# A planner that orders a two-layer trunk: later readiness times for TensorE's operands and for buffers in layer 1, and later first GpSimd transfers

## The chip, the cores and the metric

The kernel runs on one core of a Trainium2 chip. The metric is device time in microseconds of one execution, as a median over runs. The engines are called as in the profile: PE (TensorE, matmuls), PEld (its weight loads), DVE (VectorE), ACT (ScalarE), POOL (GpSimd) and SP (SyncE, which issues most transfers).

## What is computed

Two layers over 512 rows of 1024 features. Each layer is an adaptively modulated norm, a mixer with one input projection, a SiLU gate, an output projection and a gated residual. Layer 0 mixes by retention (4 heads), layer 1 by forgetting attention (16 heads of 64). A last RMS norm closes the trunk. The reference, cut to this:

```
for i in range(DEPTH):                      # DEPTH = 2
    shift, scale, gate = split(silu(c) @ mod_w[i] + mod_b[i], 3)
    h = rms_norm(x, norm_g[i]) * (1 + scale) + shift
    y = retention(h, ...) if i % 3 == 0 else forgetting_attention(h, ...)
    x = x + gate * y
return rms_norm(x, final_g)

# forgetting_attention, for each block of 128 queries
q = rms_norm(q, q_gain) * HD**-0.5;  k = rms_norm(k, k_gain)
cum = cumsum(log_sigmoid(f + b_f))
logits = q @ k.T + cum[q] - cum[k]          # causal
o = softmax(logits) @ v
y = (o * silu(g)) @ w_out
```

## The kernel before

The work is written as a program of operations (`trunk`), but it isn't emitted in the order in which it is written. Every call on an engine goes through `Proxy` and `Sched.add`, which makes a `Task` with its engine, its dependences on earlier tasks (found from the parts of buffers that are read and written), an estimated `cost` and a priority. The priority is TensorE's summed cost so far plus an offset that the program sets with `at`. When all tasks exist, `Sched.order` plays them through an event model and records the order in which they start; `emit` then issues the instructions in this order, all from line 472. On the chip each engine works through its own queue in that order, and semaphores hold what isn't ready. So the model's times decide only the order on each engine and which buffer slot a tile gets; a wait on the chip lasts as long as it really lasts.

The model, in `order`:

- Each engine takes, of its ready tasks, the one of lowest priority number whose new buffers fit. A task becomes ready when its last dependence is done plus a latency: `LAT` = 0.2 us across engines, 0 on TensorE itself, 0.13 us on another engine itself.
- Buffers are slots of a few physical pools: 60 of 512 columns ("C"), 14 of 1024 ("B"), 4 of 2048 ("G"), 24 tiny ones ("T") and the 8 PSUM banks ("Z"). Each kind of buffer has its own limit, for instance 4 banks of kind `r` (transposes, scores, values of a head) and 6 of kind `p` (projections). A slot is free again at the moment in which the last user ends.
- Costs are formulas, such as 0.069 + n / 960 us for VectorE on two inputs, 0.052 + n / 1200 (and 0.042 for a source in SBUF) for ScalarE, and n / 2260 for a matmul of n columns. A matmul of over 192 columns costs double in the model if fewer than 3072 columns were streamed in the tick (3.41 us) before.
- A transfer issued by POOL begins 0.6 us after its issue has ended, and one after the other: it is done 1.4 us and its bytes at 360 GB/s later. Transfers by SP share one modelled stream.
- In the opening, TensorE gets filler matmuls of constant ones (`filler`, tile `s` from `ones_r`) whenever it has nothing ready, until the first real product needs that bank. The fillers are real instructions on the chip.

The program around it: POOL first loads `crow` (the vector c), `vrow` (norm gains and modulation biases, three transfers) and `inv`. TensorE transposes `crow` for `csilu` and `vrow` for `vecs`, then x, and the first modulation weights are multiplied as they land; the first q and k projections of layer 0 follow. Layer 0's heads and output projection take up to about 400 us. Then come layer 1's norm, its projections of v, q and k, and the heads.

A head of layer 1 goes from engine to engine: `stacks` transposes the normalised q and k (`qn`) into PSUM, ScalarE and VectorE make stacked operands `st` from it (POOL copies some of them across partitions), `scores` multiplies them, VectorE adds the mask and the forget term (`lg`, with `ck`), ScalarE takes the exponential, POOL scales, `turn` transposes the probabilities, ScalarE and VectorE split them in two parts (`ph`), and `values` multiplies them with v into `oT`. `merge` and `zip2` interleave these steps with the remaining projections (tile `p`), whose weights come as `raw` and are split into `wh` (ScalarE) and `wl` (VectorE); `h2`, the normalised input, has the name `big`. `merge` sets the priorities only; the planner decides. After the last head, 192 matmuls of the output projection follow (tile `a`), and the final norm.

Of the kernel before, what the change touches and what calls it, by code (L numbers as in the profile page):

```python
# [26 lines left out]
PE = mybir.EngineType.PE  # L27
# [34 lines left out]

GATE1 = "q k v g0"

LOOK = 30.0

LAST = (1, 2, 3)
# [1 line left out]
N_C, N_B = 60, 14  # L69

START, TICK, TICK_COLS = 0.65, 10.24 / 3, 3072
KINDS = {
# [124 lines left out]
class Sched:  # L197
# [117 lines left out]
    def order(self):  # L315

        import heapq
        tasks = self.tasks
        free = {k: list(range(n)) for k, (n, _) in self.phys.items()}
        used = {k: 0 for k in self.kinds}  # L320
        turn = {k: 0 for k in self.kinds}
        avail = {e: [] for e in self.ENG.values()}
        busy = {e: True for e in avail}
        ev, count, out, table = [(START, 0, -i, e, None) for i, e in enumerate(busy)], 0, [], None
        hw = dma = reach = 0.0
        soft, soft_wait, soon = [], [], []
        ticks = {-1: 0}
        left = sum(t.eng == "PE" for t in tasks)
        for t in tasks:
            t.wait, t.ready = len(t.deps), 0.0  # L330
            if not t.wait:
                heapq.heappush(avail[t.eng], (t.prio, t.seq, t))

        def fits(t):
            if t.eng == "SP" and t.prio > reach:
                return False
            need = {}
            t.new = [b for b in t.bufs if b.slot is None and b.kind is not None]
            for b in t.new:
                ph, cap = self.kinds[b.kind]  # L340
                need[ph] = need.get(ph, 0) + 1
                if turn[b.kind] != b.seq or used[b.kind] >= cap or len(free[ph]) < need[ph]:
                    return False
            return True

        now = 0.0
        while True:
            moved = True
            while moved:
                moved = False  # L350
                for e in avail:
                    if busy[e]:
                        continue
                    held, got = [], None
                    while avail[e]:
                        x = heapq.heappop(avail[e])
                        if fits(x[2]):
                            got = x[2]
                            break
                        held.append(x)  # L360
                    for x in held:
                        heapq.heappush(avail[e], x)
                    if got is not None and e == "DVE" and now < LOOK and any(
                            x.prio < got.prio - 1.0 and x.ready < now + 0.2 and fits(x) for x in soon):
                        heapq.heappush(avail[e], (got.prio, got.seq, got))
                        continue
                    if got is None and e == "PE" and now > 1.5 and self.idle is not None and self.idle.buf.slot is not None:

                        got = self.filler()
                    if got is None:  # L370
                        continue
                    moved = True
                    if self.idle is not None and e == "PE" and not got.filler and self.idle.buf in got.bufs:
                        self.idle = None
                    for b in got.new:
                        ph = self.kinds[b.kind][0]
                        b.slot = free[ph].pop(0)
                        used[b.kind] += 1
                        turn[b.kind] += 1
                    out.append(got)  # L380
                    got.start = now
                    if e == "PE":
                        tick = int(now / TICK)
                        if ticks.get(tick - 1, 0) < TICK_COLS and got.cols > 192:
                            got.cost *= 2.0
                        tick = int((now + got.cost) / TICK)
                        ticks[tick] = ticks.get(tick, 0) + got.cols
                    if e == "PE":
                        left -= not got.filler or got is self.first
                        reach = max(reach, got.prio) if left else now + 1e9  # L390
                    busy[e] = True
                    count += 1
                    end = now + got.cost
                    if got.table not in (None, table):
                        end += 1.3
                        table = got.table
                    heapq.heappush(ev, (end, 0, count, e, None))
                    if got.bytes:
                        if e == "POOL":
                            soft.append(got)  # L400
                            a = end + 0.6
                        else:
                            hw = max(hw, now + 0.05) + 0.45
                            a = hw + 0.6
                        heapq.heappush(ev, (a, 3, count, None, got))
                    else:
                        got.done = end
                        heapq.heappush(ev, (end, 1, count, None, got))
            if not ev:
                break  # L410
            now = ev[0][0]
            while ev and ev[0][0] <= now:
                _, what, _, e, t = heapq.heappop(ev)
                if what == 0:
                    busy[e] = False
                elif what == 3 and t.eng == "POOL" and t is not soft[0]:

                    soft_wait.append(t)
                elif what == 3:
                    dma = max(now, dma) + t.bytes / 360e3  # L420
                    t.done = dma + 0.5
                    if t.eng == "POOL":
                        t.done = now + t.bytes / 360e3 + 1.4
                    count += 1
                    heapq.heappush(ev, (t.done, 1, count, None, t))
                elif what == 1:
                    if t.bytes and t.eng == "POOL":
                        soft.pop(0)
                        if soft and soft[0] in soft_wait:
                            count += 1  # L430
                            soft_wait.remove(soft[0])
                            heapq.heappush(ev, (now, 3, count, None, soft[0]))
                    for b in t.bufs:
                        b.users -= 1
                        if b.users == 0 and b.kind is not None:
                            free[self.kinds[b.kind][0]].append(b.slot)
                            used[b.kind] -= 1
                    for s in t.next:
                        lat = self.LAT if t.eng != s.eng else 0.0 if t.eng == "PE" else 0.13
                        s.ready = max(s.ready, t.done + lat)  # L440
                        s.wait -= 1
                        if not s.wait:
                            count += 1
                            heapq.heappush(ev, (s.ready, 2, count, None, s))
                            if s.eng == "DVE":
                                soon.append(s)
                else:
                    if t in soon:
                        soon.remove(t)
                    heapq.heappush(avail[t.eng], (t.prio, t.seq, t))  # L450
        if ev or any(avail.values()):
            todo = {e: [(t.emit[1], [(b.kind, b.seq) for b in t.new]) for _, _, t in sorted(avail[e])[:4]]
                    for e in avail}
            raise RuntimeError(f"stuck at {now:.1f} of {len(tasks) - len(out)} tasks: {todo}, {used}, {turn}")
        self.end = now
        return out
# [98 lines left out]
def trunk(tc, x, c, positions, mod_w, mod_b, norm_g, ret_w_in, ret_w_out, fox_w_in, fox_b_f,  # L555
# [6 lines left out]
    with ExitStack() as es:  # L562
# [5 lines left out]
        psp = es.enter_context(tc.tile_pool(name="psp", bufs=1, space=PSUM))  # L568
        s = Sched(tc, KINDS, {"C": (N_C, slots), "B": (N_B, slots), "G": (4, slots), "T": (24, tiny), "Z": (8, psp)})
        V, A, G, T, SY = s.vector, s.scalar, s.gpsimd, s.tensor, s.sync  # L570
# [1315 lines left out]
```

## Time and profile before

| | |
|---|---|
| median of 3 runs | 714.42 us (714.22 to 714.66) |
| the profiled execution | 714.6 us, span 712.6 us |
| instructions | 10207, of them 3383 matmuls |
| HBM | 113.35 MB read, 4.25 MB written |
| granted TensorE clock, mean | 0.998 |

The span runs from the first to the last instruction; the time of the execution holds some more around it. "Busy" of an engine is the union of its instructions' bars. The chain of waits goes back from the last instruction, at each step to what released it. A bracket behind an instruction of the timeline gives its engine's idle time before it and what ended it. All operations have the line 472, so groups are told apart by tiles: out<-in.

### The profile page before, as it was taken

To read this page: it belongs to the slowest core of one execution; us is meant where nothing else is said; L and a number is where in the kernel's file an instruction comes from. 1 tells how busy PE (TensorE), PEld (TensorE's weight loads), DVE (VectorE), ACT (ScalarE), POOL (GpSimd) and SP (SyncE) were. 2 spreads that over 40 slices of the span, in tenths; PEclk is the share of its full clock that TensorE was granted. 3 is DMA by queue.
4 is the path that set the end of the run, shared out by engine and by line. 5 is a ranking of instruction groups with operands and counts; after the bars stand their busy time and mean duration, and the time that the engine had idled before them with its cause. 6 is when DMAs were issued, how large, how long until landed. Compare 5 with 4: busy or idle time off the path is not lost.

```text
span 712.6 us, 10207 instructions
## 1 busy us (share of the span) xinstructions
PE 700.3 (98%) x3383; PEld 576.7 (81%) x3383; DVE 617.5 (87%) x1268; ACT 420.2 (59%) x779; POOL 128.0 (18%) x175
## 2 busy tenths in 40 slices
PE   8999999999999999999999999999999999999995
PEld 6888888888888888888888887787877888888884
DVE  4799999888978996998998899699898998789925
ACT  5558564654365435865534565674777677779613
POOL 1001101100010001001000102014463564442011
PEclk9999999999999999999999999999999999999999
DMA  8992964647666766717669315668776696757002
GB/s 285 349 327 86 183 211 82 140 164 265 128 152 206 236 121 158 269 60 147 186 203 296 147 41 118 126 210 196 202 165 169 178 214 152 184 132 232 36 14 104
DMA packets 80724, 122.47 MB, mean 172 GB/s; under 512 B 7080, under 2 KB 39968, under 8 KB 80672
## 3 DMA queue, kind: packets, MB, share of 16 engines
q1 hardware_dynamic: 66176, 98.71, 43.2%
q0 software_dynamic: 14496, 23.10, 19.0%
q8 instruction: 27, 0.44, 0.3%
q14 instruction: 25, 0.20, 0.1%
HBM read 113.35 MB, written 4.25 MB: 165 GB/s over the span
## 4 chain that ended last, share of the span: by engine, by line
PE 82%; DVE 12%; ACT 3%; issue 2%; DMA 0%; POOL 0%; DVEq 0%; ACTq 0%; POOLq 0%
PE p L472 48%; PE r L472 17%; PE a L472 11%; PE s L472 6%; DVE wl L472 2%; DVE t L472 2%; DVE st L472 1%; DVE qn L472 1%; DVE xn L472 1%; DVE lg L472 1%; DVE ph L472 1%; ACT st L472 1%; ACT lg L472 1%; ACT wh L472 1%; DVE x L472 1%
## 5 line engine op out<-in xcount | busy, mean ns | idle before, releaser
L472 DVE TENSOR_TENSOR wl<-raw,wh 128x1024 fp32r<-128x1024 f32 x132 | 160.5, 1219 | 27.8 <-PE p L472 16.2
L472 ACT CAST wh<-raw 128x1024 fp32r<-128x1024 f32 x132 | 137.3, 1051 | 76.7 <-PE p L472 37.7
L472 PE MATMUL p<-wh,big 128*128 128x512 f32 x304 | 102.8, 400 | 0.0
L472 PE MATMUL p<-wh,sf 128*128 128x512 f32 x320 | 101.6, 392 | 0.0
L472 PEld LDWEIGHTS p<-wh,sf 128*128 128x128 f32 x320 | 60.0, 188 | 12.8
L472 PEld LDWEIGHTS p<-wh,big 128*128 128x128 f32 x304 | 56.8, 189 | 10.7
L472 POOL DMA_DIRECT2D raw<-in_ret_w_in x16 | 19.4, 1212 | 255.9 <-DMA raw<-in_mod_w 78.2
L472 PE MATMUL p<-wh,act 128*128 128x512 f32 x192 | 62.7, 393 | 0.0
L472 PE MATMUL p<-wl,sf 128*128 128x512 f32 x160 | 62.7, 392 | 0.0
L472 PE MATMUL p<-wl,big 128*128 128x512 f32 x152 | 60.7, 400 | 0.0
L472 POOL TENSOR_SCALAR lg<-lg,t 128x512 f32<-128x512 f32 (+1 forms) x64 | 46.9, 838 | 67.5 <-DVE t L472 64.5
L472 DVE SCALAR_TENSOR_TENSOR macc<-raw,csilu,macc 128x512 f32<-128x512 f32 x76 | 57.1, 753 | 0.8
L472 PE MATMUL p<-act,wh 128*128 128x512 f32 x160 | 53.4, 393 | 0.0
L472 ACT ACTIVATE lg<-lg,t 128x512 f32<-128x512 f32 (+1 forms) x64 | 35.7, 559 | 13.8 <-DVE t L472 13.5
L472 PE MATMUL p<-big,wh 128*128 128x512 f32 x128 | 43.6, 403 | 0.0
L472 PE MATMUL r<-act,sh 128*128 128x512 f32 x120 | 42.7, 391 | 0.2 <-DVE sh L472 0.2
L472 PEld LDWEIGHTS p<-wh,act 128*128 128x128 f32 x192 | 36.0, 188 | 7.3
L472 PE MATMUL p<-wh,go 128*128 128x512 f32 x112 | 39.2, 402 | 0.0
L472 PE MATMUL p<-wl,act 128*128 128x512 f32 x96 | 37.8, 394 | 0.0
L472 PEld LDWEIGHTS p<-wl,sf 128*128 128x128 f32 x160 | 30.0, 188 | 6.1
L472 PE MATMUL r<-st,st 128*128 128x512 f32 (+3 forms) x128 | 34.1, 337 | 0.5 <-DVE st L472 0.3
L472 PEld LDWEIGHTS p<-act,wh 128*128 128x128 f32 x160 | 29.8, 188 | 5.6
(213 smaller groups left out, 1592.9 us busy)
## 6 DMA issues: line engine op xcount, KB each, us to landing
raw<-in_ret_w_in SPq DMA_DIRECT2D x48, 512.0 KB, 5.3
raw<-in_mod_w SPq DMA_DIRECT2D x64, 256.0 KB, 6.0
raw<-in_fox_w_in SPq DMA_DIRECT2D x32, 512.0 KB, 4.6
raw<-in_ret_w_in POOLq DMA_DIRECT2D x16, 512.0 KB, 6.4
raw<-in_mod_w SPq DMA_DIRECT2D x16, 512.0 KB, 4.4
raw<-in_ret_w_out SPq DMA_DIRECT2D x16, 512.0 KB, 4.9
ck<-cum_dram SPq DMA_DIRECT2D x16, 448.0 KB, 4.8
x<-in_x SPq DMA_DIRECT2D x16, 256.0 KB, 5.9
```

The lines of the kernel that those rows point to most:

```text
L472: getattr(eng, op)(*[real(v) for v in args], **{k: real(v) for k, v in kw.items()})
```

## The change

Five constants come in. `order` uses them in four places: the tick that decides on the doubled cost gets a phase (0.0); a POOL transfer that the model issues before 5 us begins `FIRST` = 1.0 us later; after model time `MARGIN_FROM` = 420 us a buffer is free `FREE` = 0.5 us after its last user's end, by an event of its own; and after that time a TensorE task whose dependence ran on another engine (or is a transfer) becomes ready `MARGIN` = 0.8 us later. The program `trunk`, its operations, buffers and priorities are the same.

```
+MARGIN, FREE, MARGIN_FROM = 0.8, 0.5, 420.0
...
+PHASE, FIRST = 0.0, 1.0
...
                     if e == "PE":
-                        tick = int(now / TICK)
+                        tick = int((now - PHASE) / TICK)
                         if ticks.get(tick - 1, 0) < TICK_COLS and got.cols > 192:
                             got.cost *= 2.0
-                        tick = int((now + got.cost) / TICK)
+                        tick = int((now + got.cost - PHASE) / TICK)
...
                         if e == "POOL":
                             soft.append(got)
-                            a = end + 0.6
+                            a = end + 0.6 + (FIRST if now < 5.0 else 0.0)
...
+                elif what == 4:
+                    free[self.kinds[t.kind][0]].append(t.slot)
+                    used[t.kind] -= 1
...
                         if b.users == 0 and b.kind is not None:
-                            free[self.kinds[b.kind][0]].append(b.slot)
-                            used[b.kind] -= 1
+                            count += 1
+                            heapq.heappush(ev, (now + (FREE if now > MARGIN_FROM else 0.0), 4, count, None, b))
                     for s in t.next:
                         lat = self.LAT if t.eng != s.eng else 0.0 if t.eng == "PE" else 0.13
+                        if s.eng == "PE" and t.eng != "PE" and now > MARGIN_FROM:
+                            lat += MARGIN
```

## The prediction

> **What bounds the kernel now.** I read the page first, then the chain of waits, then the groups of TensorE's matmuls by shape in the stage from 480 to 660 us, then who waited for whom.
>
> ```profile
> span 712.6 us, 10207 instructions
> PE 700.3 (98%) x3383; PEld 576.7 (81%) x3383; DVE 617.5 (87%) x1268; ACT 420.2 (59%) x779; POOL 128.0 (18%) x175
> ...
> PE 82%; DVE 12%; ACT 3%; issue 2%; DMA 0%; POOL 0%; DVEq 0%; ACTq 0%; POOLq 0%
> ...
> L472 DVE TENSOR_TENSOR wl<-raw,wh 128x1024 fp32r<-128x1024 f32 x132 | 160.5, 1219 | 27.8 <-PE p L472 16.2
> L472 ACT CAST wh<-raw 128x1024 fp32r<-128x1024 f32 x132 | 137.3, 1051 | 76.7 <-PE p L472 37.7
> ```
>
> TensorE is busy 98% of the span, and no other engine is full. The chain still goes through VectorE for 12% of it, so somewhere TensorE's pace is set by VectorE. The next two fences say where: three rows of the chain, then the stage that holds layer 1's heads.
>
> ```profile
> 419.24 13.42 PE p L472 x59
> ...
> 657.34 4.39 PE p L472 x19
> 661.73 42.89 PE a L472 x192
> ```
>
> ```profile
> 480.00:660.00 180.00, 177.42 (x948) 146.16 (x947) 160.52 (x386) 132.02 (x303) 83.97 (x126) 1.00 0.72 184
> ```
>
> In the chain, 59 matmuls of 512 columns took 13.42 us, 0.2275 us each, and 192 at the end 42.89 us, 0.223 each: where nothing disturbs TensorE, that is the pitch. The columns of the window are TensorE, weight loads, VectorE, ScalarE, GpSimd. TensorE looks idle for only 180 - 177.42 = 2.6 us. But a matmul's bar is longer than its pitch, as the next rows show (mean 404 ns), so a short wait hides under the bar before it. What the 948 matmuls should take is counted by shape (of eight groups of 32, the first and the last stand here; the others have 512, 384, 384, 256, 256 and 128 columns):
>
> ```profile
> L472 PE MATMUL p<-wh,big 128*128 128x512 f32 x188 | 65.5, 404 | 0.0
> L472 PE MATMUL p<-big,wh 128*128 128x512 f32 x124 | 42.4, 403 | 0.0
> L472 PE MATMUL p<-wl,big 128*128 128x512 f32 x94 | 38.0, 404 | 0.0
> L472 PE MATMUL r<-ident,lg 128*128 128x128 f32 x160 | 28.5, 274 | 1.1 <-DVE st L472 0.4 <-DVE oT L472 0.3 <-DVE t L472 0.3
> L472 PE MATMUL p<-big,wl 128*128 128x512 f32 x62 | 25.3, 409 | 0.0
> L472 PE MATMUL r<-ph,v 128*128 128x512 f32 x32 | 13.4, 418 | 0.6 <-ACT ph L472 0.5
> ...
> L472 PE MATMUL r<-ident,qn 128*128 128x128 f32 x60 | 9.8, 274 | 0.4 <-DVE qn L472 0.4
> ...
> L472 PE MATMUL r<-ph,v 128*128 128x128 f32 x32 | 5.7, 250 | 0.0
> L472 PE MATMUL r<-mh,ones_r 128*128 128x512 f32 x4 | 1.2, 391 | 0.0
> ```
>
> ```profile
> 12.85 1.75 PE p L472 x16
> ```
>
> A transpose costs 1.75 / 16 = 0.109 us. The 512-column matmuls are 188 + 124 + 94 + 62 + 64 + 4 = 536, at 0.2275: 121.9 us. The 64 each of 384, 256 and 128 columns, priced by their columns at 0.171 + 0.114 + 0.057: 21.8. The 220 transposes: 24.1. Together 167.8 us, in a stage of 180. So TensorE loses **12.2 us** in this stage, not 2.6. VectorE is busy 160.5 of the 180 us, with 19.5 us to spare. [...]
>
> **The change, part by part.** Nothing is computed differently. The kernel's order on every engine is made by the event model in `order`, and the change makes that model more pessimistic in three places, so only the order of instructions moves. The tick phase is 0.0 and changes nothing.
>
> *Operand margin, 0.8 us, from model time 420.* A TensorE task whose operand comes from another engine or a transfer counts as ready 0.8 us later; the planner then gives TensorE something else that is ready, nearly always projection matmuls (the `p` rows). No wait instruction is added: a task that was ready anyway is only emitted behind three or four projection matmuls (0.8 / 0.2275 = 3.5). These are the waits that TensorE's records show from 420 on:
>
> ```profile
> PE r L472 <- DVE st L472: 0.6, 2, 0.4
> PE r L472 <- ACT ph L472: 0.5, 2, 0.3
> PE r L472 <- DVE qn L472: 0.4, 1, 0.4
> PE r L472 <- DVE oT L472: 0.3, 1, 0.3
> PE r L472 <- DVE t L472: 0.3, 1, 0.3
> PE r L472 <- ACT z L472: 0.3, 1, 0.3
> ```
>
> ```profile
> 489.62 0.39 PE L472 MATMUL p<-wh,big 128*128 128x512 f32 x1
> 490.38 1.15 PE L472 MATMUL r<-ident,qn 128*128 128x128 f32 x8 [0.38 <-DVE qn L472]
> ...
> 525.22 0.39 PE L472 MATMUL p<-wl,big 128*128 128x512 f32 x1
> 525.95 0.30 PE L472 MATMUL r<-ident,lg 128*128 128x128 f32 x1 [0.35 <-DVE oT L472]
> ...
> 634.53 0.50 PE L472 MATMUL r<-ph,v 128*128 128x512 f32 x1 [0.32 <-ACT ph L472]
> 634.87 0.39 PE L472 MATMUL r<-st,st 128*128 128x512 f32 x1
> ```
>
> Eight waits, 2.4 us of visible idle. At 489.62 the next matmul could have started at 489.85; it started at 490.38, so 0.53 us is lost where 0.38 is shown. At 525.22 it is 0.50 for 0.35. With 0.15 more for each, the eight cost 2.4 + 1.2 = 3.6 us. All are shorter than 0.8, and a projection stands just before the first two, so other work is at hand. I take two thirds as gone: 2.4 us; the bounds are 0 and 3.6. The rest of the 12.2 us, some 9.0 (3.6 less the one wait before 480 us is 3.2), lies in pieces too short for the view to name. One kind is seen at 634.53: the matmul there is followed after 0.34 us, 0.11 more than the pitch, because the weights behind a wait come late too. A margin acts on such near misses as on waits, but switches between shapes stay. Bounds 0 and 9.0; I take a quarter, 2.2 us, near the low end, since no row says which of them are waits.
>
> *Buffer margin, 0.5 us, from 420.* A buffer whose last user ended counts as free 0.5 us later, so TensorE's next user of a PSUM bank, a transfer into a `raw` buffer or a VectorE result is planned later. The wait at 525.95 looks like that kind: a transpose wants a bank that `oT`'s reader releases, 0.50 us late. Its gain is within the 2.4. Its price is bank time: a head uses four banks for scores, four for turning, one for values and one for its share of the stacks, so 16 heads take 160 uses (the 160 `lg` transposes are ten a head); 160 x 0.5 = 80 us out of four `r` banks x 180 = 720, or 11%. Transfers issued 0.5 us later are not what this stage waits for (no transfer stands in the waits above). I price it at 0, with the heads' rival below as its upper bound.
>
> *Later first transfers of GpSimd.* For the five small transfers that GpSimd issues in the first 5 us the model adds 1.0 us to their start, so filler matmuls are planned where TensorE now waits for `crow`.
>
> ```profile
> 1.31 3.38 DMA crow<-in_c
> ...
> 5.07 4.99 PE s L472 x11
> ...
> 10.33 2.52 PE s L472 x10
> ```
>
> ```profile
> 4.83 0.24 PE L472 MATMUL r<-ident,crow 8*128 8x8 f32 x1 [0.59 <-DMA crow<-in_c]
> ...
> 5.17 0.18 ACT L472 ACTIVATE csilu<-r 128x8 f32<-128x8 f32 x1 [1.09 <-PE r L472]
> ...
> 10.13 0.72 ACT L472 ACTIVATE x<-x,t 128x512 f32<-128x512 f32 x1 [0.47 <-DVE t L472]
> ...
> 12.69 1.91 PE L472 MATMUL p<-ident,x 128*128 128x128 f32 x16
> ```
>
> TensorE waits 0.59 us for `crow`, then runs 11 fillers at 0.45 us, then 10 at 0.25, and starts on x at 12.69, though the first normalised piece was done at 10.85. So the fillers, not x, hold it, by up to 1.84 us. If two or three fillers move from behind `crow` to ahead of it, the 0.59 us is used and x starts that much earlier. ScalarE's `csilu` follows `crow`: it is planned a microsecond later as well, behind one more square of x, and since ScalarE now stands 1.09 us before it and the squares behind it wait for x's landing anyway, that costs 0. GpSimd's five transfers keep their order. What is late next is the weights: transfers of `mod_w` and the first projections keep the queues full.
>
> ```profile
> 20.00:40.00 20.00, 20.00 (x119) 17.31 (x119) 16.70 (x26) 9.40 (x12) 0.00 (x0) 1.00 1.10 349
> ```
>
> With 1.10 of the DMA engines' time taken at 349 GB/s, little of an earlier start survives to 60 us. I take half of the 0.59, a gain of 0.3. Bounds: 1.6 us gained (next part) and 1.0 lost, if the whole added microsecond becomes fillers and none is dropped later. A new opening also shuffles layer 0's order; TensorE has no idle worth the name there, so that can lose some tenths and gain nothing; 0, within these bounds.
>
> *Sum.* The profiled execution took 714.6, 2.0 us beyond its span of 712.6, and lies within the runs (714.22 to 714.66), 0.2 above their median. 714.4 - 2.4 - 2.2 - 0.3 = **709.5 us**.
>
> **The rivals.** *VectorE is the limit, and the waits move (713.4).* The model's `cost` gives the 1024-column subtraction 0.069 + 1024 / 960 = 1.136 us, and the row says 1.219; the cast gets 0.947 and takes 1.051. So VectorE and ScalarE fall behind the plan by 7 to 11%. A margin of 0.8 us is used up after about 0.8 / 0.083 = 10 us of work without a pause; from there each wait comes back as before. For it: VectorE's 12% of the chain. Against it: 19.5 us of pauses in 180, one us in nine, which would still be 14.7 if the stage shrank by 4.8. Then 1.0 us is gained.
>
> *The heads become too slow (717.9).* A head passes to TensorE four times (normalised q and k, stacked operands, probabilities, turned probabilities): 4 x 0.8 = 3.2 us more planned latency a head. It decides when the projections that fill the time run out. Now 19 projection matmuls, 4.39 us, stand behind the last `r` (657.34 in the chain), and they are the reserve. If half the latency of each of the last eight heads is not overlapped, 1.6 x 8 = 12.8 us is due, 4.4 is covered, 8.4 is paid against 4.9 gained: 3.5 us slower. Against it: two heads are in flight, and the planner takes late heads first by priority whenever they are ready.
>
> *The clock is released a step earlier (708.2).* In the rows above, a filler costs 0.45 us up to 10 us and 0.25 after. If the gap at `crow` is what keeps TensorE from full rate until 10 us, closing it makes some eight fillers 0.20 us cheaper: 1.6 us, less than the 1.84 by which x is early, in place of the 0.3. [...]
>
> *It does nothing (714.4)*: if the ready tasks' priorities leave no choice. With 476 of the 948 matmuls being transposes, scores and values between projections, that is hardly so.
>
> **How the numbers follow.** Forecast 0.58, clock 0.14, VectorE 0.14, heads 0.12, nothing 0.02. About 0.2%, 1.43 us, is what a measurement of this kernel can tell from no change: faster is below 713.0, slower above 715.9. The VectorE case with its opening bounds straddles 713.0, so 0.04 of it goes to faster: faster 0.58 + 0.14 + 0.04 = 0.76; same 0.10 + 0.02 = 0.12; slower 0.12. The range reaches down to all eight waits, half of the small pieces and the opening's full gain, 714.4 - 3.6 - 4.5 - 1.6 = 704.7, and up to no gain with the spread of the runs, 714.6. It leaves out the heads' rival and a little below: 2 in 10.
>
> **What would show it.** Right: from 480 us to the start of the last 192 `a` matmuls the same matmuls take about 4.5 us less than now, the waits on `st`, `qn`, `ph` and `oT` are gone or below 0.2 us, and VectorE's busy time is unchanged in less span. The wait on `crow` is gone with more fillers ahead of it. Wrong: the stage keeps its length with waits under other names (VectorE); no `p` stands between the last `r` and the `a` matmuls, and waits gather there (heads); or layer 0 has new waits that its order did not have.

## The result, and the profile after

Median 709.54 us (709.24 to 710.38, 4 runs) against 714.32 us (713.92 to 714.66, 4 runs) on the same chip: ratio 0.9937, 95% interval 0.9925 to 0.9949, or 4.5 us less by the ratio. The forecast was 709.5. The profiled execution took 710.38 us with a span of 708.4.

The page after, its rows on the span, the engines and the chain:

```profile
span 708.4 us, 10215 instructions
PE 696.1 (98%) x3383; PEld 575.8 (81%) x3383; DVE 616.8 (87%) x1268; ACT 419.8 (59%) x779; POOL 127.4 (18%) x175
...
PE 90%; DVE 4%; DMA 2%; ACT 1%; issue 1%; SPq 1%; DVEq 0%; ACTq 0%
```

The work is the same (3383 matmuls, 616.8 us of VectorE). TensorE's share of the chain rose from 82% to 90%, VectorE's fell from 12% to 4%: fewer of TensorE's starts hang on VectorE. The chain, at the places shown of the kernel before:

```profile
418.86 13.42 PE p L482 x59
...
655.45 1.67 PE p L482 x7
657.12 42.89 PE a L482 x192
```

From the 59 projection matmuls to the 192 `a` matmuls it is 657.12 - 418.86 = 238.26 us, where it was 661.73 - 419.24 = 242.49. The span is 4.2 us shorter, and this stretch alone makes that up. Another 0.38 was won ahead of it, and 0.4 lost at the end: from the first `a` matmul to the span's end it took 708.4 - 657.1 = 51.3 us, and 50.9 before, with the same 42.89 us of `a` matmuls. Only 7 projection matmuls, 1.67 us, stand behind the last `r`, where 19 stood.

Who waited for whom on TensorE, the whole span after:

```profile
PE r L482 <- DMA raw<-in_mod_w: 1.4, 1, 1.4
PE s L482 <- DVE ones_r L482: 1.3, 1, 1.3
PE r L482 <- DVE ph L482: 0.6, 2, 0.3
PE r L482 <- DVE st L482: 0.5, 2, 0.3
PE r L482 <- DMA vrow<-in_mod_b: 0.5, 1, 0.5
PE r L482 <- DVE sh L482: 0.2, 1, 0.2
```

From 420 us on there are four waits of 1.1 us (`ph` and `st`) instead of eight of 2.4. The place at which the transposes of `qn` waited 0.38 us looks like this now, in TensorE's timeline:

```profile
488.81 0.39 PE L482 MATMUL p<-wh,big 128*128 128x512 f32 x1
489.08 1.09 PE L482 MATMUL r<-ident,qn 128*128 128x128 f32 x8
```

0.27 us after the projection, no bracket. The window of the heads, columns as before:

```profile
480.00:656.00 176.00, 174.82 (x943) 146.17 (x942) 158.68 (x383) 129.48 (x300) 82.81 (x125) 1.00 0.72 184
```

VectorE still pauses 17.3 of 176 us: it didn't become the limit. The opening, TensorE's rows of the timeline:

```profile
1.32 3.68 PE L482 MATMUL s<-ones_r 128*128 128x512 f32 x8 [1.32 <-DVE ones_r L482]
...
4.93 0.22 PE L482 MATMUL r<-ident,crow 8*128 8x8 f32 x1
...
5.08 3.47 PE L482 MATMUL s<-ones_r 128*128 128x512 f32 x14
...
9.00 0.23 PE L482 MATMUL r<-ident,vrow 48*128 48x48 f32 x1 [0.46 <-DMA vrow<-in_mod_b]
...
10.43 1.96 PE L482 MATMUL p<-ident,x 128*128 128x128 f32 x16
...
22.23 0.71 PE L482 MATMUL r<-csilu,raw 128*128 128x128 f32 x4 [1.45 <-DMA raw<-in_mod_w]
```

Eight fillers now fill the wait for `crow`. The 14 behind it take 0.25 us each, not 0.45: the clock was released (a granted clock of 1.0 begins) at 4.75 us of the span, and at 10.36 before. x is begun 2.26 us earlier (10.43 for 12.69). Then TensorE waits 1.45 us for `mod_w`, and the first product of the start comes at 23.84 instead of 24.33.

### The profile page after: what moved, and what is told of

It reads as the page before. It is cut to its first block, busy times and chain, and to the rows that moved or that the text cites. A ratio compares the mean times of both kernels' runs of the same rounds, so it can differ in the third digit from the quotient of the medians.

```text
span 708.4 us, 10215 instructions
## 1 busy us (share of the span) xinstructions
PE 696.1 (98%) x3383; PEld 575.8 (81%) x3383; DVE 616.8 (87%) x1268; ACT 419.8 (59%) x779; POOL 127.4 (18%) x175
## 4 chain that ended last, share of the span: by engine, by line
PE 90%; DVE 4%; DMA 2%; ACT 1%; issue 1%; SPq 1%; DVEq 0%; ACTq 0%
PE p L482 56%; PE r L482 17%; PE a L482 12%; PE s L482 5%; DMA raw<-in_mod_w 2%; DVE st L482 1%; SPq L482 1%; ACT st L482 1%; DVE ph L482 0%; DVE macc L482 0%; DVE t L482 0%; DVE lg L482 0%; DVE wl L482 0%; DVE qn L482 0%; ACT ph L482 0%
## 5 line engine op out<-in xcount | busy, mean ns | idle before, releaser
L482 PE MATMUL p<-wh,big 128*128 128x512 f32 x304 | 99.9, 398 | 0.0
L482 POOL TENSOR_SCALAR lg<-lg,t 128x512 f32<-128x512 f32 (+1 forms) x64 | 41.0, 671 | 72.6 <-DVE t L482 67.5
L482 DVE TENSOR_TENSOR ph<-r,ph 128x128 fp32r<-128x128 f32 (+1 forms) x64 | 30.6, 483 | 3.8 <-ACT ph L482 3.2
```

Of the source, the lines that this page charges most:

```text
L482: getattr(eng, op)(*[real(v) for v in args], **{k: real(v) for k, v in kw.items()})
```

## The experiments

Each time stands beside runs of the kernel before on the same chip, and the ratio is to these: their median was 714.61 us beside the four kernels that take the change apart ("opening alone" to "both margins"), 714.32 beside "tiny margin", "half", "double" and "costs instead", and 714.15 beside the last four. "Stage" is the time from the first projection on layer 1's input to the first `a` matmul, "left" the number of projection matmuls behind the last values, "clock" the moment at which full rate was granted, each from the one profile of the kernel.

| kernel | operand, buffer, first | median us | ratio to before (95%) | stage us | left | clock us |
|---|---|---|---|---|---|---|
| before | 0, 0, 0 | 714.32 | 1 | 252.74 | 19 | 10.36 |
| changed | 0.8, 0.5, 1.0 | 709.54 | 0.9937 (0.9925 to 0.9949) | 248.47 | 7 | 4.75 |
| opening alone | 0, 0, 1.0 | 713.64 | 0.9988 (0.9979 to 0.9997) | 252.67 | 19 | 5.59 |
| operand alone | 0.8, 0, 0 | 712.28 | 0.9967 (0.9955 to 0.9980) | 250.65 | 5 | 9.86 |
| buffer alone | 0, 0.5, 0 | 713.31 | 0.9981 (0.9970 to 0.9991) | 251.17 | 28 | 5.97 |
| both margins | 0.8, 0.5, 0 | 710.16 | 0.9935 (0.9923 to 0.9947) | 248.47 | 7 | 9.90 |
| tiny margin | 0.05, 0, 1.0 | 712.95 | 0.9980 (0.9971 to 0.9989) | 252.30 | 22 | 4.64 |
| half | 0.4, 0.5, 1.0 | 709.01 | 0.9930 (0.9918 to 0.9941) | 248.68 | 16 | 10.56 |
| double | 1.6, 0.5, 1.0 | 714.05 | 0.9996 (0.9987 to 1.0005) | 251.04 | 0 | 7.19 |
| costs instead | 0, 0, 1.0 | 714.74 | 1.0001 (0.9989 to 1.0014) | 251.49 | 0 | 6.11 |
| half, from 60 | 0.4, 0.5, 1.0 | 714.81 | 1.0012 (1.0004 to 1.0021) | 247.83 | 16 | 5.20 |
| half, first earlier | 0.4, 0.5, -1.0 | 711.32 | 0.9964 (0.9952 to 0.9977) | 248.13 | 16 | 8.31 |
| buffer doubled | 0.4, 1.0, 1.0 | 710.82 | 0.9957 (0.9944 to 0.9971) | 249.05 | 0 | 4.91 |
| 1.6, then 0.4 | 1.6/0.4, 0.5, 1.0 | 709.02 | 0.9930 (0.9917 to 0.9942) | 248.02 | 16 | 6.50 |

Where nothing is left, the stage looks too short: the first `a` matmul then comes ahead of the last seven or eight products of probabilities and values. From the stage's start to the span's end it is 303.8 us before, 299.9 in the changed kernel, 304.1 in "double", 306.5 in "costs instead" and 301.6 in "buffer doubled".

The theory: the plan ran TensorE's consumers so close behind their producers that small delays added up to much of the 12.2 us; slack in the plan absorbs them, as long as projections are left to fill it. The rivals: the model's low costs; luck of a new order; the opening.

**The parts, one at a time.**

```
-MARGIN, FREE, MARGIN_FROM = 0.8, 0.5, 420.0
+MARGIN, FREE, MARGIN_FROM = 0.0, 0.0, 420.0
```

> Only the 1.0 us for GpSimd's first transfers; both margins are 0. TensorE's order differs from the kernel before in the opening alone: fillers 8, 14 and 5 instead of 6, 11 and 10. Theory (the opening and layer 1 are separate gains): about 0.4 us faster than before, since the first product comes earlier by 0.5 us at most and waits for mod_w in between; the waits of layer 1 are as in the kernel before, and its stage is as long. Rival (the clock released a step earlier is worth its whole 1.6 us): 712.7. Second rival (a shift of the opening alone changes layer 1): the stage from the 59 projection matmuls to the a matmuls changes by over 0.5 us.

0.12% faster (0.03 to 0.21), 0.2 to 1.5 us: twice the 0.4 expected. The stage is unchanged, 252.67 us, and TensorE's order differs from before in the fillers alone. The opening of this kernel:

```profile
5.22 0.24 PE L482 MATMUL r<-ident,crow 8*128 8x8 f32 x1
5.39 3.58 PE L482 MATMUL s<-ones_r 128*128 128x512 f32 x14
```

The clock was released at 5.59 us, and the first product came at 22.91, 1.4 us earlier than before. Up to 0.47 us of this is the shorter wait for `crow` (0.12 us in the trace for 0.59); the rest goes with the earlier clock. Opening and layer 1 are separate.

```
-MARGIN, FREE, MARGIN_FROM = 0.8, 0.5, 420.0
+MARGIN, FREE, MARGIN_FROM = 0.8, 0.0, 420.0
-PHASE, FIRST = 0.0, 1.0
+PHASE, FIRST = 0.0, 0.0
```

> Only the operand margin of 0.8 us from 420 us; buffers free at once, opening as before. Theory (late operands are the larger part): 710.9, some 3.5 us faster, waits on st, qn and ph gone or below 0.2 us, while a wait for a bank (as on oT at 526) remains. Rival (the bank margin carries the gain): within 1 us of the kernel before.

The stage is 2.1 us shorter, not 3.5, and the waits of layer 1 are these:

```profile
PE r L482 <- DVE st L482: 2.0, 4, 0.9
PE r L482 <- POOL lg L482: 0.3, 1, 0.3
PE r L482 <- DVE t L482: 0.3, 1, 0.3
```

Six waits with 2.6 us of idle, as much as the 2.4 before. `qn`, `ph` and `oT` are gone, `oT` against expectation, and `st` has more than tripled. So this margin alone gained nothing in the waits that the view names; all of its 2.1 us are in pieces that lie below it.

```
-MARGIN, FREE, MARGIN_FROM = 0.8, 0.5, 420.0
+MARGIN, FREE, MARGIN_FROM = 0.0, 0.5, 420.0
-PHASE, FIRST = 0.0, 1.0
+PHASE, FIRST = 0.0, 0.0
```

> Only the buffer margin of 0.5 us from 420 us. Theory: 713.5, some 0.8 us faster; the transposes that waited for a bank no longer do, the waits for st, qn and ph stay. Rival (the bank margin carries the gain, or any new order of layer 1 does): 711 or less.

1.6 us off the stage, and the waits on `qn`, `oT`, `t` and `z` are gone:

```profile
PE r L482 <- DVE st L482: 1.0, 3, 0.4
PE r L482 <- ACT ph L482: 0.6, 2, 0.3
```

The buffer margin is no small part: 1.6 beside the operand margin's 2.1. That `qn`, an operand, lost its wait shows that a name doesn't tell which margin will help: each margin moves everything behind it.

```
-PHASE, FIRST = 0.0, 1.0
+PHASE, FIRST = 0.0, 0.0
```

> Both margins from 420 us, opening as before. From TensorE's first product on, its order is that of the changed kernel. Theory (opening and layer 1 add up): 710.0, that is 0.4 us slower than the changed kernel. Rival (the opening carries more): 711 or more.

The median is 710.16, the number of the theory, but beside its own runs of the kernel before it is no slower than the changed kernel: the ratios are 0.9935 and 0.9937. The opening's 0.4 us is too small for these two intervals to show. The stage is 248.47 us, the same as in the changed kernel to the last digit. Together the margins give 4.27 us, a little more than their sum of 3.7.

**Slack, or any new order?**

```
-MARGIN, FREE, MARGIN_FROM = 0.8, 0.5, 420.0
+MARGIN, FREE, MARGIN_FROM = 0.05, 0.0, 420.0
```

> FIRST as in the changed kernel, operand margin 0.05 us from 420 us, no buffer margin: over half of the order of layer 1 on TensorE differs from the kernel before, but nothing has slack to speak of. Theory (slack is what pays): as with FIRST alone, 713.6 on the scale of the first batch; the stage from the first product on h2 to the a matmuls stays at 252 to 253 us. Rival (any new order of layer 1 is better, since the old one was an unlucky draw): 251.5 or less, and 712.5.

The stage moved by 0.37 us against the opening alone, and the ratios 0.9980 and 0.9988 overlap. This order, new but without slack, gains a tenth of what the margins give, while all six kernels with both margins and projections left at the end have stages of 247.8 to 248.7 us: luck isn't a likely cause. One such order was run, so it isn't excluded either.

**How much slack.**

```
-MARGIN, FREE, MARGIN_FROM = 0.8, 0.5, 420.0
+MARGIN, FREE, MARGIN_FROM = 0.4, 0.5, 420.0
```

> Operand margin halved to 0.4 us, the rest as in the changed kernel. Theory (slack covers waits up to its size; of the waits before, five of eight cost more than 0.4 us): the stage takes 249.5 to 251, the time is 711. Rival (a margin pays by its being there): 248.5 and 709.7.

The theory said 711, and it is 709.01: half the margin does as much, with a stage only 0.2 us longer and 16 projections left. The sizes of the named waits were the wrong measure of the slack that is needed.

```
-MARGIN, FREE, MARGIN_FROM = 0.8, 0.5, 420.0
+MARGIN, FREE, MARGIN_FROM = 1.6, 0.5, 420.0
```

> Operand margin doubled to 1.6 us, the rest as in the changed kernel. Theory (no wait before was longer than 0.54 us, so the second 0.8 us buys nothing): 248 to 249.5 for the stage, 709 to 710.5. Rival (VectorE's lag grows until it has used any slack up): a further 1 us or more faster. Rival (the heads become too slow): no projection is left behind the last values, and 712 or more.

714.05: the rival of the slow heads came true. In the windows of this kernel the loss is in one place, behind 640 us; the timeline names it:

```profile
620.00:640.00 20.00, 20.00 (x114) 17.07 (x113) 18.08 (x45) 15.36 (x35) 10.56 (x17) 1.00 0.68 168
640.00:660.00 20.00, 16.56 (x91) 14.24 (x90) 19.37 (x50) 16.41 (x41) 8.73 (x10) 0.91 0.65 210
```

```profile
654.37 0.51 PE L482 MATMUL r<-ph,v 128*128 128x512 f32 x1 [2.48 <-ACT ph L482]
```

TensorE has no idle from 620 to 640 us and 3.44 in the next 20, and waits 2.48 us for one head's probabilities with nothing else to do. The granted clock, third column from the end, fell to 0.91 there as well: it stood at 0.5 from 655.72 to 659.13 us, which is worth about 1.7 us (estimated as half of the 3.41).

```
-                            lat += MARGIN
+                            lat += MARGIN if now < 560.0 else 0.4
```

(with `MARGIN` = 1.6)

> Operand margin 1.6 us from 420 to 560 us of model time and 0.4 after, buffer margin 0.5. Theory (1.6 us lost only because the heads fell behind and the projections ran out before the last values): projections are again left behind the last values, the loss between 640 and 660 us is below 2 us, the stage takes 248 to 249.5, 709 to 710. Rival (so long a margin loses on the way too, by banks or by late heads): 250 or more, 711.5.

As the theory said: 16 projections are left, the stage takes 248.02 us, and the same window holds

```profile
640.00:660.00 20.00, 20.00 (x107) 16.80 (x106) 18.45 (x37) 19.03 (x39) 2.89 (x4) 1.00 0.73 226
```

no idle at all. So 1.6 us did its harm only by using the reserve up, and up to 560 us it gained little over 0.4 (248.02 for 248.68).

```
-MARGIN, FREE, MARGIN_FROM = 0.8, 0.5, 420.0
+MARGIN, FREE, MARGIN_FROM = 0.4, 1.0, 420.0
```

> Operand margin 0.4, buffer margin doubled to 1.0 us. Theory (0.5 us already covers the bank waits; more only holds banks): stage 248.5 to 250 us, 709 to 710.3. Rival (VectorE's lateness in freeing banks is the larger part): 247.5 or less, 708. Rival (banks run out): 711 or more.

710.82 lies between the 710.3 of the theory and the 711 of the rival of the banks, and its interval (0.9944 to 0.9971, some 710.2 to 712.1 us) covers both. Nothing is left behind the last values, and the output projection waits for its gated operand:

```profile
PE a L482 <- ACT goh L482: 1.5, 1, 1.5
```

A longer buffer margin draws on the same reserve as the operand margin.

**The costs instead.**

```
+                    if now > MARGIN_FROM and not got.bytes:
+                        got.cost *= {"DVE": 1.08, "ACT": 1.1}.get(e, 1.0)
```

(both margins 0)

> No margins; instead the model's costs of VectorE and ScalarE are multiplied by 1.08 and 1.10 from 420 us, about what the rows show over the formulas; FIRST as in the changed kernel. Theory (slack covers lateness of any source, and a transfer or semaphore is late as often as an engine): half of the gain, a stage of 250 to 251.5 and 711.5. Rival (the waits came from costs that are too low, and are gone with the right ones): 248.5 or less and 709.7 or less.

714.74, with runs from 711.4 to 716.0. The plan leaves nothing behind the last values, and this trace waits there: in the stretch of 3.41 us from 654.64 us TensorE is idle for 1.52, and from 658.05 to 664.88 us the granted clock is 0.5. The output projection then starts at half rate:

```profile
661.47 44.42 PE a L484 x191
```

```profile
661.80 1.05 PE L484 MATMUL a<-wh,goh 128*128 128x512 f32 x2
662.66 0.63 PE L484 MATMUL a<-wl,goh 128*128 128x512 f32 x1
```

Two matmuls from 661.80 to 662.66 are 0.43 us each, and the 191 took 44.42 us, 1.8 more than at the pitch of 42.89 / 192: about what 3.41 us at half clock cost, 1.7. Not every run pays this. The mean granted clock was 0.992 in the three runs from 715.5 to 716.0 us, and 0.998 in those of 711.40, 711.84 and 713.49.

Up to there the costs did most of the margins' work. With the matmuls begun in the first 230 us of the stage counted at the prediction's prices (0.2275 us for 512 columns, by columns for fewer, 0.109 for a transpose), TensorE had lost 13.3 us before, 13.3 with the tiny margin, 10.8 here and 9.9 in the changed kernel and in "half". So nearer costs gave 2.5 of the margins' 3.4 us and then ran out of projections. That the waits come from costs that are too low is not excluded: the run ends no faster because of the reserve and the clock.

**Where the margins begin.**

```
-MARGIN, FREE, MARGIN_FROM = 0.8, 0.5, 420.0
+MARGIN, FREE, MARGIN_FROM = 0.4, 0.5, 60.0
```

> Margins 0.4 and 0.5 us from model time 60 us instead of 420, so layer 0 is planned with them too; opening as in the changed kernel. Theory (slack pays where TensorE waits, and layer 0 has two waits of note, together some 0.6 us): 0 to 0.8 us faster than with the same margins from 420 us, 708.2 to 709.0, and the stretch up to the first product on h2 is at most 0.8 us shorter. Rival (the margins do harm where there is nothing to win, hence 420): 710 or more.

The rival holds. The stage is the shortest of all, 247.83 us, but layer 1's input comes at 414.57 us instead of 408.93. The waits between 60 and 420 us:

```profile
PE p L482 <- DVE oa L482: 1.4, 1, 1.4
PE a L482 <- ACT wh L482: 1.2, 1, 1.2
PE p L482 <- DVE wl L482: 1.1, 1, 1.1
PE a L482 <- DVE wl L482: 0.5, 1, 0.5
```

Layer 0 had one wait of 0.2 us there and has 4.2 us now, for weights and bank readers at the output projection. Two of them idle TensorE for 2.2 of the 3.41 us from 356.78 us, and the granted clock is 0.5 for the next 3.41, some 1.7 us more by the estimate above. With nothing to win, the margin only moved work to where TensorE has no filler.

**The opening.**

```
-PHASE, FIRST = 0.0, 1.0
+PHASE, FIRST = 0.0, -1.0
```

(margins 0.4 and 0.5)

> GpSimd's first transfers planned 1.0 us earlier instead of later, margins 0.4 and 0.5 us from 420 us: fillers 4, 9 and 14, the same 27, so TensorE waits longer for crow. Theory (the opening's gain is the clock, released early when no gap stands in its window): release after 8 us, the first product at 24 us or later, about 1 us slower than the same margins with FIRST = 1.0, 710. Rival (the gain is a chance of the run's phase, and FIRST has no part in it): release before 7 us or the same 709.0.

0.34% slower than the same margins with +1.0 (711.32 and 709.01, on two chips; ratios 0.9964 and 0.9930), more than twice what was expected.

```profile
5.07 0.24 PE L482 MATMUL r<-ident,crow 8*128 8x8 f32 x1 [1.68 <-DMA crow<-in_c]
5.24 3.75 PE L482 MATMUL s<-ones_r 128*128 128x512 f32 x9
```

TensorE waits 1.68 us, the clock is released at 8.31 us, and the first product comes at 24.39, both as the theory said. The two profiled runs don't differ, though, for that of "half" was released late as well: they took 710.54 and 710.63 us, the fastest of five runs here and the slowest of five there. Over all 14 profiles, the nine with a release before 7.2 us have their first product between 22.49 and 23.84 us, the five others between 24.07 and 24.43. The nine early ones show at most 0.25 us of idle on TensorE before `crow`, the five late ones 0.38 us or more. `FIRST` makes the early release likely, not sure: with 1.0 us eight of nine profiles have it, with 0 one of four, with -1.0 the one doesn't. "Half" was released at 10.56 after a gap of 0.38 us, since `crow` was used late (5.48); "buffer alone", without `FIRST`, was released at 5.97 after a gap of 0.25, since `crow` came early (4.50).

## Why the prediction was right, by its steps

*The 12.2 us.* This was the step that carried it. From the stage's start to the first `a` matmul, the visible idle of TensorE fell from 2.91 us to 1.22, while the stage became 4.27 us shorter: 2.6 us of the gain lay under the bars, as the count by pitch had it.

*Named waits, 2.4 forecast.* Eight waits became four, 2.4 us of idle became 1.1; with 0.15 more for each wait, 3.6 became 1.7: 1.9 us. `qn` and `oT` are gone as forecast, `st` and `ph` still wait up to 0.3 us. *Small pieces, 2.2 forecast:* what remains of the stage's 4.27 is 2.4. The sum is right, and both parts are near, but the shares that gave them (two thirds, a quarter) were choices that no row supported.

*Which margin does what* was wrong. The forecast had the named waits going with the operand margin, and the buffer margin's gain within them. Alone, the operand margin took 2.1 us off the stage with as much named idle as before, and the buffer margin took 1.6 off. That the wait on `oT` is a wait for a bank isn't shown: it went with either.

*Price of the buffer margin, 0.* At 0.5 us no run shows one. At 1.0 us the reserve was gone, and the kernel lost 0.27% against 0.5 us (ratios 0.9957 and 0.9930). The 11% of bank time did not tell this.

*The opening, 0.3 forecast.* The gain went with what the rival named, the clock (released at 4.75 us in the changed kernel's profile, at 10.36 before); the size isn't settled. The fillers moved as forecast, 8, 14 and 5 for 6, 11 and 10. In the changed kernel's profile the first product came 0.49 us earlier and layer 1 began 0.35 us earlier, since 1.45 of the 2.26 us went to the wait for `mod_w`, the thing named as late next. Alone the change is worth 0.2 to 1.5 us, and the 14 profiles put some 1.3 us between early and late release (means 23.0 and 24.3 at the first product), but between "both margins" and the changed kernel the medians show nothing. An early release goes with at most 0.25 us of idle before `crow` (nine profiles), a late one with 0.38 us or more (five); that this gap decides is the author's estimate from these 14, and what else moves the release, from 4.64 us ("tiny margin") to 10.56 ("half"), was not shown. The forecast expected a shuffle of layer 0 as well; there was none.

*VectorE as the limit* didn't happen: it pauses 17.3 of 176 us, where 14.7 of 175 was the forecast's figure. *The slow heads* did, at 1.6 us, in the forecast's own way: the reserve of 19 matmuls fell to 7 at 0.8 us and to 0 at 1.6. At 0.8 us, 1.67 of the 4.39 us were left.

That 709.5 came out to 0.04 us is luck. In the profiled run the parts give 4.2 us (714.6 to 710.4) where 4.9 was forecast: 4.27 from the stage, 0.35 ahead of it, and 0.4 lost behind the last arithmetic. That loss is the same, 0.43 us, in the profile of "both margins", whose order on TensorE is the same from the first product on, and in no other plan that kept projections in reserve; its cause stays open. The median lies 0.84 us below the profiled run, and no trace shows a run that fast.

No version is clearly faster than the changed kernel: "half" (0.9930, 0.9918 to 0.9941) and "1.6, then 0.4" (0.9930, 0.9917 to 0.9942) overlap with its 0.9937 (0.9925 to 0.9949). Both leave 16 projections in reserve instead of 7.

## What to carry to other kernels

Measure an in-order engine's loss by pitch (counts by shape times the undisturbed price), not by its idle column; here 12.2 us stood behind 2.6. Slack in a static order pays where other work is at hand to fill it, a small dose gives nearly all of it, and the work left behind the last dependent step tells how much more can be spent. Where TensorE ran dry, the loss was more than the wait in three of the profiles: the granted clock stood at 0.5 behind it for 3.41 us in "double" and in "half, from 60", and for 6.83 in "costs instead". Change one margin at a time, because the names of the waits don't tell which margin removes them.

## What the runs showed of the hardware that was not expected

The moment of the clock's release differs by 6 us between profiles of nearly the same opening (4.64 us in "tiny margin", 10.56 in "half"), and 0.38 us or more of TensorE's idle before `crow` goes with all the late ones.

In the heads and the output projections the granted clock fell to 0.5 in three profiles, each time behind waits of TensorE: at 655.72 us in "double", behind 2.48 us for `ph` and 0.46 for `lg`; at 360.19 in "half, from 60", behind 1.18 us for `wh` and in the last 0.03 of 1.42 for `oa`; at 658.05 in "costs instead", behind 0.62, 0.23 and 0.67 us, together 1.52. The wait of 1.45 us for `mod_w` in the changed kernel's profile did not lower it: there the granted clock is 1.0 from 4.75 to 704.49 us. How much idle it takes was not shown; the ends of the bars, from which idle is counted, are modelled.

The first small transfer by GpSimd, issued at 1.3 us of the span, landed 3.0 us later in the changed kernel's profile, 3.4 before and 4.0 in "half": a spread as large as the correction that the change makes.
